# The second layer's conditioning map in a fused two-layer backbone kernel: products on ScalarE, sums of eight on GpSimd, the sum over partitions on TensorE

## The chip, the core and the metric

The kernel runs on one core of one Trainium2 chip. The metric is the device time of one execution in microseconds (us). The engines are named as the profile names them: PE is TensorE (PEld its weight loads), DVE is VectorE, ACT is ScalarE, POOL is GpSimd, SP is SyncE, which here only issues DMAs. "ACTq" is ACT's instruction queue: DMAs that ACT issues stand there, in order with its other work.

## The reference, cut to what matters

The program is one inference step of a two-layer backbone of width 1024, over 1024 latent and 128 context tokens. Each layer has a mixer (a convolution and Fourier mixer in layer 0, an S5 scan in layer 1) and a gated feed forward part; both are modulated by shift, scale and gate vectors, which come from the conditioning vector through one linear map per layer:

```
mod = jax.nn.silu(c_in) @ p['w_ada'][l] + p['b_ada'][l]      # (2 vectors, 1024) @ (1024, 6144)
sh1, sc1, g1, sh2, sc2, g2 = jnp.split(mod[:, None, :], N_MOD, axis=-1)
h = modulate(rmsnorm(x, p['norm1_g'][l]), sh1, sc1)           # h * (1 + scale) + shift
...                                                           # mixer, h -> m
x = x + g1 * m
h = modulate(rmsnorm(x, p['norm2_g'][l]), sh2, sc2)
x = x + g2 * swiglu(h, p['w_ffn_in'][l], p['w_ffn_out'][l])
```

There are two conditioning vectors: one for the latent tokens, one for the context tokens. The change concerns `mod` of the second layer (l = 1) and nothing else of the computation.

## The kernel before, in words

All products of activations and weights go through three fp32r matmuls of 384 columns on PE (`mm3`, lines 120 to 125): a weight tile is read by a DMA of SP's queue into `wraw`, ACT rounds it to `whi` (line 116), DVE takes the rest `wlo` (line 117), each with two buffers, and PE multiplies high by high, high by low and low by high. Results lie in six PSUM banks, which ACT or DVE empty.

Layer 0's feed forward is `ffn` (from line 603). `inner(j)` makes two weight tiles `wg` and `wu` and, for each of three chunks of 384 tokens, 24 matmuls with each; ACT takes silu of the first (line 619), DVE multiplies by the second (line 621), and the product is split in two (lines 153, 154). `outer(j0)`, after each second `inner`, multiplies back and DVE adds to the residual (line 599). The last pair, `last_outer`, goes a chunk at a time, so that the norm and then the modulated input of the S5 layer (`S5In.chunk`, lines 1020 to 1026, on ACT with shift and scale of layer 1) can start chunk by chunk.

Two other pieces of work ride along in `ffn`. They are a generator, `fill`: first the S5 tables' constants (`Tables.build`, 41 steps), then `table_steps` (from line 835), 8 tiles of 4 batches with 11 steps each and a step of `prepare` per tile, 360 steps. These are mostly short DVE operations with both inputs in SBUF (lines 831 to 833). `pump` (in `ffn`) advances the generator in proportion to the matmuls issued: 425 times the share of the work done. By the end of the loop over j that share is (4608 - 144) / 4752 = 0.94, so 400 steps have been taken; what is left is issued at once, ahead of `at_end()` and `last_outer`.

Inside the batches, layer 1's conditioning map is computed. Every seventh step `ada_rows` (lines 310 to 318) multiplies one block of 128 outputs: eight fp32 matmuls, 32 columns of `cond` (the two conditioning vectors, padded) stationary and 128 weight columns moving, four groups of products side by side. ACT copies the block's result to `arow`, issues its store to memory, and issues the load of the next block (`ada_load`, line 294, 512 KB in one buffer). After every six blocks `ada_sums` (lines 320 to 329) has ACT issue eight small DMAs, which bring the rows back as one output per partition, and POOL adds the four groups and the bias, giving `modt[1]`. There are 48 blocks and 8 sums. When the generator ends, POOL makes `scale_t[1]` (`ada_scale`, lines 332 and 334, called in lines 1726 and 1727).

Layer 0 has most of its own map computed the other way, in `ada_slice` (lines 265 to 284), before the feed forward: one product per slice and vector on ACT (line 274), the other seven accumulated on DVE (line 276), a matmul with `ones32` for the sum over partitions (line 280), rows through memory (line 284), `ada_columns` (lines 286 to 290) to bring them back.

What sets the order: within the program text, the order of the generators' steps. A planner then lays out every engine's instructions when the kernel is built, with program order as the priority; an instruction whose inputs or buffers are not ready in the plan lets later ones go ahead. On the chip each engine runs its list in order and waits where an input is late.

Of the kernel before, what the change touches and what calls it, by code (L numbers as in the profile page):

```python
# [38 lines left out]
SLOT = 8 * W  # L39


def segments(lo, hi):
    """the parts of a range of tokens by conditioning."""
    out = []
    if lo < LAT:
        out.append((lo, min(hi, LAT), 0))
    if hi > LAT:
        out.append((max(lo, LAT), hi, 1))
    return out
# [7 lines left out]
def kernel(  # L57
# [30 lines left out]
    # ---------------------------------------------------------------- constants  # L88
# [7 lines left out]
    ada1_d = dram.tile([128, 48 * 128], F32, name="ada1_d")  # L96
# [11 lines left out]
    # ---------------------------------------------------------------- helpers  # L108
# [24 lines left out]
    class Pools:  # L133
# [9 lines left out]
        def s(self, p, dt=F32):  # L143
            """short-lived tiles, apart from the long-lived ones where they have slots of their own."""
            return self.act.tile([128, CW], dt, tag="s", name=nm(p), bufs=self.ns) if self.ns else self.a(p, dt)
# [11 lines left out]
    # rsqrt(v) by Newton from an integer seed  # L157
# [17 lines left out]
    def unpermuted(fn, dst, src, ch):  # L175
        """context tokens back from (t, c) order."""
        if ch < NCH - 1:
            return fn(dst, src)
        n = LAT - ch * CW
        fn(dst[:, :n], src[:, :n])  # L180
        fn(dst[:, n:].rearrange("p (c t) -> p c t", t=T8), src[:, n:].rearrange("p (t c) -> p c t", t=T8))

    class Norm:
        """means of squares of a chunk's tokens, three blocks of tokens with one per partition."""
# [28 lines left out]
    def spread(r):  # L213
        """rstd of three blocks of tokens from a column per block to every partition."""
        rb, bw = aux("nrb"), r.shape[0]
        for j in range(3):
            PE.transpose(rb[:, j * bw:(j + 1) * bw], r[:, j:j + 1].to_broadcast([bw, 128]), ident[:bw, :bw])
        return rb

    def modulated_tile(P, x, rb, f, ch, l, which):  # L220
        """x * rstd * scale + shift of a tile, in its two parts; rb covers the chunk."""
        t, hi, lo = P.t("t"), P.h("hh", F32R), P.h("hl", F32R)
        c0 = ch * CW
        for a, b, s in segs(ch):
            cs = slice(a - c0, b - c0)
            sh = modt[l][:, 24 * which + f, s:s + 1]
            V.scalar_tensor_tensor(t[:, cs], x[:, a:b], scale_t[l][:, which, f, s:s + 1], rb[:, cs], op0=OP.mult, op1=OP.mult)
            S.activation(hi[:, cs], t[:, cs], AF.Identity, bias=sh)
            V.scalar_tensor_tensor(lo[:, cs], t[:, cs], sh, hi[:, cs].bitcast(F32), op0=OP.add, op1=OP.subtract)
        return hi, lo  # L230

    def modulated(P, norm, ch, xs, l, which, h):
        """in parts, a tile each."""
        rb = norm.scale(ch)
        for f in range(NF):
            h[f][ch] = modulated_tile(P, xs[f], rb, f, ch, l, which)
            yield
# [4 lines left out]
    # ---------------------------------------------------------------- conditioning  # L242
# [22 lines left out]
    def ada_slice(P, s):  # L265
        """a slice of layer 0's conditioning map, off the tensor engine but for the sum over partitions;
        in two parts, to be issued some time apart. The rows go through memory to one feature per partition."""
# [18 lines left out]
    def ada_columns(l, b0, nb, src, t):  # L286
        """blocks of 128 outputs, from memory to one per partition."""
        for i in range(2):
            nc.scalar.dma_start(t[:, i, :], src[i].rearrange("(b c) -> c b", c=128))
        V.tensor_add(modt[l][:, b0:b0 + nb, :], t.rearrange("p s b -> p b s"), vec_a[:, 48 * l + b0:48 * l + b0 + nb, None].to_broadcast([128, nb, 2]))  # L290
# [6 lines left out]
    def ada_block(pool, l, s, raw, nrow=2):  # L297
        """in two parts, to be issued some time apart."""
# [11 lines left out]
    def ada_rows(pool, s, raw):  # L310
        """a block of layer 1's conditioning map, the rows of the four groups of products to memory."""
        ps = aux("ada")
        for k in range(8):
            j = k % 4
            PE.matmul(ps[32 * j:32 * j + 32, :128], cond[:, k, :], raw[:, k, :], start=(k < 4), stop=(k >= 4))
        row = pool.tile([128, 128], F32, tag="arow", name=nm("arow"), bufs=2)
        S.activation(row, ps[:, :128], AF.Copy)
        nc.scalar.dma_start(ada1_d[:, s * 128:s * 128 + 128], row)

    def ada_sums(pool, b0, nb):  # L320
        """sums of the four groups, one output per partition."""
        t = pool.tile([128, 4, 2, nb], F32, tag="acol", name=nm("acol"), bufs=2)
        for j in range(4):
            for i in range(2):
                nc.scalar.dma_start(t[:, j, i, :], ada1_d[32 * j + i, b0 * 128:(b0 + nb) * 128].rearrange("(b c) -> c b", c=128))
        G.tensor_add(t[:, 0:2], t[:, 0:2], t[:, 2:4])
        G.tensor_add(t[:, 0], t[:, 0], t[:, 1])
        G.tensor_add(modt[1][:, b0:b0 + nb], t[:, 0].rearrange("p s b -> p b s"),
                     vec_a[:, 48 + b0:48 + b0 + nb, None].to_broadcast([128, nb, 2]))
# [13 lines left out]
    # ---------------------------------------------------------------- entry  # L343
    def start(P, st, x, h):
        """x to one feature per partition, its norm, modulation and the first two tiles of the
        input projection, a feature tile at a time as the conditioning arrives."""
# [96 lines left out]
    # ---------------------------------------------------------------- layer 0 mixer  # L443
    def mixer(P, big, x, h, norm2, hn, first):
# [10 lines left out]
        def four_in(i):  # L455
# [5 lines left out]
            # folded about 512 and 256: sums of even and odd outputs for cosine, then sine, and the middle  # L461
# [140 lines left out]
    # ---------------------------------------------------------------- feed forward  # L602
    def ffn(P, l, x, h, norm_next, steps=None, nsteps=0, at_end=None, per_chunk=None):
# [32 lines left out]
        def last_outer(j0):  # L636
            """the last two, a chunk of tokens at a time."""
# [25 lines left out]
    # ---------------------------------------------------------------- S5 tables  # L663
# [10 lines left out]
    def exp_poly(pool, x, n):  # L674
        """exp of an fp32 array by range reduction and a polynomial."""
# [21 lines left out]
    def sincos(pool, a, n):  # L697
        """sine and cosine of an fp32 array, reduced by parts of 2 pi that multiply exactly."""
# [36 lines left out]
    def state_layout(dst0, dst1, dup):  # L735
        """[(d, p), g] from dup[(d, g), p twice]."""
# [98 lines left out]
    def table_steps(P, pool, tb):  # L835
# [149 lines left out]
        raw, ns, summed, turn = ada_load(pool, 1, 0), 0, 0, 0  # L985
        for f in range(8):
            ct = prepare(f, *nxt)
            yield
            for q in range(4):
# [4 lines left out]
                for i, _ in enumerate(batch(f, q, ct, both)):  # L994
                    if ns % 6 == 0 and turn % 7 == 5 and summed < ns:
                        ada_sums(pool, summed, 6)
                        summed = ns
                    if turn % 7 == 0 and ns < 48:
                        ada_rows(pool, ns, raw)
                        ns += 1  # L1000
                        if ns < 48:
                            raw = ada_load(pool, 1, ns)
                    turn += 1
                    yield

    # ---------------------------------------------------------------- S5 layer
    class S5In:
        """modulated input of the S5 layer, a chunk of tokens at a time."""
# [24 lines left out]
    class S5:  # L1033
# [40 lines left out]
        def parts(f):  # L1074
            """the first and the last tile go through in halves."""
# [52 lines left out]
        def front(self, f):  # L1128
            """input products, chunk sums."""
# [43 lines left out]
        def back(self, f):  # L1173
            """outputs of the states, back to one feature per partition."""
# [73 lines left out]
    # ---------------------------------------------------------------- layer 1 after the scan  # L1248
# [6 lines left out]
    class Glu:  # L1255
        """gated output projection of the scan's outputs, half of the tokens at a time, in quarters."""
# [23 lines left out]
        def late(self, ws, cc):  # L1280
            """products of the first output, those with the last of the scan's outputs at the end."""
# [43 lines left out]
        def modulate(self, c):  # L1325
            """in place and in parts, a tile each."""
# [55 lines left out]
    class Fast:  # L1382
        """feed forward input product by seven products of half the features, tokens and outputs of a pair;
        for the first pair of outputs by eight."""
# [22 lines left out]
        def forms(self, s, h1, h2, tmp, eng):  # L1407
            """what the products take of two quarters of the tokens; in parts."""
# [40 lines left out]
        def weights(self, r):  # L1449
            """the seven weights in the order of the products."""  # L1450
# [43 lines left out]
        def plain(self, s, work):  # L1494
            """the first two outputs of half of the tokens."""
# [61 lines left out]
        def steps(self, j, up, tiles):  # L1557
            """a step per product of the outputs j and j + 1."""
# [8 lines left out]
            def done(n, s, src):  # L1567
                """an output to the hidden features."""
# [43 lines left out]
    class FfnOut:  # L1612
        """feed forward output product, a chunk of tokens at a time."""
# [85 lines left out]
    # ---------------------------------------------------------------- program  # L1699
# [138 lines left out]
```

## Time and profile before

| what | value |
|---|---|
| median of 3 runs (lowest to highest) | 2558.5 us (2555.06 to 2559.73) |
| profiled execution: its span, first to last instruction | 2550.3 us |
| what lies between that span and the median | 8.2 us |
| stage of the change (from the first load of layer 1's map to the end of the loop over j) | 480 to 1262 us of the span |
| handover to the S5 layer | 1262 to about 1320 us |

The profile gives, for one execution, when each engine was busy and what it waited for. Two things matter in reading it. The duration of a matmul is a modelled one and successive matmuls overlap, so that PE's pace is read from the distance between starts. And DVE and POOL instructions show longer durations when they were held up after they started, so a duration that is far above its usual value is a wait as well.

### The profile page before, as it was taken

The numbers are of one execution on the slowest core, as the hardware profiler recorded it, in microseconds if no ns is written. First come the engines' busy times: TensorE is split into PE (matmuls) and PEld (weight loads), VectorE is DVE, ScalarE is ACT, GpSimd is POOL, SyncE is SP. The second block draws the span as 40 slices with busy tenths as digits, with TensorE's granted clock in tenths as the row PEclk, the third lists the DMA queues.
The fourth block names the chain that finished last, engine by engine and source line by source line (L and its number), as shares of the span: only waits on it lengthen the run. The fifth ranks groups of instructions, "written<-read, shape, count | busy, mean of one in ns | idle before, by whom it ended". The sixth has DMA issues, their size and how long they took to land. (4 is left out here: it accounts for less than half of the span.)

```text
span 2550.3 us, 44262 instructions
## 1 busy us (share of the span) xinstructions
PE 2426.1 (95%) x16815; PEld 2360.4 (93%) x16815; DVE 1789.7 (70%) x4641; ACT 906.2 (36%) x1915; POOL 252.0 (10%) x256
## 2 busy tenths in 40 slices
PE   7999999999999999999956789999999999989998
PEld 6999999999999999999946679998999999989998
DVE  7765678787787778887869984558766666644444
ACT  5322443233222322223364443435232232434333
POOL 0000120000000000000124421112000000122110
PEclk9999999999999999999978889999999999999999
DMA  9443342244444444443457954433222222466543
GB/s 258 127 137 96 92 116 61 68 122 122 123 115 123 122 114 130 115 131 115 116 195 221 261 177 147 120 103 103 74 77 69 88 62 86 147 204 189 162 132 124
DMA packets 503093, 327.96 MB, mean 129 GB/s; under 512 B 99144, under 2 KB 472448, under 8 KB 502880
## 3 DMA queue, kind: packets, MB, share of 16 engines
q1 hardware_dynamic: 330208, 233.10, 30.8%
q10 hardware_dynamic: 163680, 58.96, 9.6%
q0 software_dynamic: 8992, 33.07, 3.9%
q8 instruction: 133, 2.18, 0.4%
q14 instruction: 80, 0.66, 0.1%
HBM read 254.04 MB, written 71.01 MB: 127 GB/s over the span
## 5 line engine op out<-in xcount | busy, mean ns | idle before, releaser
L123 PE MATMUL mm<-hh,whi 128*128 128x384 f32 x1392 | 472.6, 339 | 1.1 <-ACT f L459 1.1
L125 PE MATMUL mm<-hh,wlo 128*128 128x384 f32 x1392 | 466.4, 335 | 0.0
L124 PE MATMUL mm<-hl,whi 128*128 128x384 f32 x1392 | 465.3, 334 | 0.0
L117 DVE TENSOR_TENSOR wlo<-wraw,whi 128x1024 fp32r<-128x1024 f32 (+1 forms) x216 | 259.8, 1203 | 243.5 <-ACT whi L116 240.2
L116 ACT ACTIVATE whi<-wraw 128x1024 fp32r<-128x1024 f32 (+1 forms) x218 | 226.0, 1037 | 506.3 <-PE mm L124 383.5
L123 PEld LDWEIGHTS mm<-hh,whi 128*128 128x128 f32 x1392 | 261.3, 188 | 11.2 <-issue 9.2
L125 PEld LDWEIGHTS mm<-hh,wlo 128*128 128x128 f32 x1392 | 261.3, 188 | 2.9 <-issue 2.5
L124 PEld LDWEIGHTS mm<-hl,whi 128*128 128x128 f32 x1392 | 261.5, 188 | 0.0
L599 DVE SCALAR_TENSOR_TENSOR xall<-mm,modt,xall 128x384 f32<-128x384 f32 (+2 forms) x416 | 203.6, 510 | 60.3 <-PE mm L125 59.4
L123 PE MATMUL mm<-hb,whi 128*128 128x384 f32 x528 | 179.9, 341 | 11.3 <-ACT whi L116 11.2
L1534 PE MATMUL mm<-T,wf 128*128 128x288 f32 x640 | 189.4, 296 | 0.0
L1535 PE MATMUL mm<-T,wf 128*128 128x288 f32 x640 | 188.8, 295 | 0.0
L1536 PE MATMUL mm<-T,wf 128*128 128x288 f32 x640 | 188.2, 294 | 0.0
L125 PE MATMUL mm<-hb,wlo 128*128 128x384 f32 x528 | 179.4, 340 | 2.0 <-DVE wlo L117 1.9
L123 PE MATMUL mm<-hidh,whi 128*128 128x384 f32 x528 | 180.0, 341 | 0.0
L124 PE MATMUL mm<-hb,whi 128*128 128x384 f32 x528 | 178.6, 338 | 0.0
L125 PE MATMUL mm<-hidh,wlo 128*128 128x384 f32 x528 | 176.6, 334 | 0.0
L124 PE MATMUL mm<-hidl,whi 128*128 128x384 f32 x528 | 176.5, 334 | 0.0
L196 POOL TENSOR_TENSOR ssq<-ssq,sq 128x384 f32<-128x384 f32 (+1 forms) x78 | 100.1, 1284 | 686.9 <-ACT sq L192 683.7
L123 PE MATMUL mm<-zz,whi 128*128 128x288 f32 x512 | 151.5, 296 | 2.4 <-ACT zz L1267 2.4
L124 PE MATMUL mm<-zz,whi 128*128 128x288 f32 x512 | 150.8, 295 | 0.3
L125 PE MATMUL mm<-zz,wlo 128*128 128x288 f32 x512 | 150.4, 294 | 0.3 <-DVE wlo L117 0.3
(391 smaller groups left out, 5710.5 us busy)
## 6 DMA issues: line engine op xcount, KB each, us to landing
wraw<-in_w_ffn_out_dram SPq DMA_DIRECT2D x70, 512.0 KB
wraw<-in_w_ffn_in_dram SPq DMA_DIRECT2D x52, 512.0 KB
araw<-in_w_ada_dram ACTq DMA_DIRECT2D x48, 512.0 KB
wraw<-in_w_glu_dram SPq DMA_DIRECT2D x32, 512.0 KB
araw<-in_w_ada_dram ACTq DMA_DIRECT2D x80, 192.0 KB
wraw<-in_w_out_mix_dram SPq DMA_DIRECT2D x24, 512.0 KB
xall<-in_w_ffn_in_dram SPq DMA_DIRECT2D x20, 512.0 KB
wr<-in_w_ffn_in_dram SPq DMA_DIRECT2D x20, 512.0 KB
```

The source lines that it names most:

```text
L116: S.activation(hi[:, :n], raw[:, :n], AF.Copy)
L117: eng.tensor_sub(lo[:, :n], raw[:, :n], hi[:, :n].bitcast(F32))
L123: PE.matmul(ps, wh, xs[0], start=start, stop=False)
L124: PE.matmul(ps, wh, xs[1], start=False, stop=False)
L125: PE.matmul(ps, wl, xs[0], start=False, stop=stop)
L196: self.last = G.tensor_add(self.ssq[ch], self.ssq[ch], sq)
L599: V.scalar_tensor_tensor(x[o][:, a:b], ps[:, a - ch * CW:b - ch * CW], gate(l, which, o, s), x[o][:, a:b], op0=OP.mult, op1=OP.add)
L1534: PE.matmul(ps, wh, xh[:, cs], start=kt == 0, stop=False)
L1535: PE.matmul(ps, wh, xl[:, cs], start=False, stop=False)
L1536: PE.matmul(ps, wl, xh[:, cs], start=False, stop=kt == NFK - 1)
```

## The change

A generator `ada_pool` takes the place of `ada_load`, `ada_rows` and `ada_sums` for layer 1. It goes over 32 slices of 192 outputs. Each slice has eight steps: a load of 128 by 192 weights (96 KB, two buffers), two products on ACT (one per conditioning vector; `Copy` with a scale per partition), and, from the second step on, two additions on POOL into the accumulators. Then four empty steps, two matmuls with `ones32` for the sum over partitions, a copy on ACT and two row stores. One step of it is taken at each step of a batch. What is left of it is drained when the batches are through, one yield each; then one `ada_columns` brings back all 48 blocks, with the addition of the bias on DVE. `pump` and its count of 425 stay as they are.

```diff
+AW = 192
...
-    ada1_d = dram.tile([128, 48 * 128], F32, name="ada1_d")
+    ada1_d = dram.tile([2, 48 * 128], F32, name="ada1_d")
...
-    def ada_rows(pool, s, raw):
...
-    def ada_sums(pool, b0, nb):
...
+    def ada_pool(pool):
+        for c0 in range(0, 48 * 128, AW):
+            acc = [pool.tile([128, AW], F32, tag="acc", name=nm("acc"), bufs=2) for _ in range(2)]
+            for k in range(8):
+                raw = pool.tile([128, AW], F32, tag="araw", name=nm("araw"), bufs=2)
+                nc.scalar.dma_start(raw, w_ada[1, k * 128:(k + 1) * 128, c0:c0 + AW])
+                for i in range(2):
+                    if k == 0:
+                        S.activation(acc[i], raw, AF.Copy, scale=cond[:, 0, i:i + 1])
+                    else:
+                        t = pool.tile([128, AW], F32, tag="aprod", name=nm("aprod"), bufs=2)
+                        S.activation(t, raw, AF.Copy, scale=cond[:, k, i:i + 1])
+                        G.tensor_add(acc[i], acc[i], t)
+                yield
+            for _ in range(4):
+                yield
+            ps = aux("ada")
+            for i in range(2):
+                PE.matmul(ps[32 * i:32 * i + 32, :AW], ones32, acc[i], start=True, stop=True)
+            row = pool.tile([128, AW], F32, tag="aprod", name=nm("arow"), bufs=2)
+            S.activation(row[0:64], ps[0:64, :AW], AF.Copy)
+            for i in range(2):
+                nc.scalar.dma_start(ada1_d[i:i + 1, c0:c0 + AW], row[32 * i:32 * i + 1])
...
-        raw, ns, summed, turn = ada_load(pool, 1, 0), 0, 0, 0
+        ada = ada_pool(pool)
...
                 for i, _ in enumerate(batch(f, q, ct, both)):
-                    if ns % 6 == 0 and turn % 7 == 5 and summed < ns:
-                        ada_sums(pool, summed, 6)
-                        summed = ns
-                    if turn % 7 == 0 and ns < 48:
-                        ada_rows(pool, ns, raw)
-                        ns += 1
-                        if ns < 48:
-                            raw = ada_load(pool, 1, ns)
-                    turn += 1
+                    next(ada, None)
                     yield
+        for _ in ada:
+            yield
+        ada_columns(1, 0, 48, ada1_d, pool.tile([128, 2, 48], F32, tag="acol", name="acol1", bufs=1))
```

## Rows read from the trace of the kernel before

**Rows 1.** The page: the span, and busy time of each engine.

```profile
span 2550.3 us, 44262 instructions
PE 2426.1 (95%) x16815; PEld 2360.4 (93%) x16815; DVE 1789.7 (70%) x4641; ACT 906.2 (36%) x1915; POOL 252.0 (10%) x256
```

**Rows 2.** Busy time by stretch: PE, PEld, DVE, ACT, POOL; granted clock, DMA.

```profile
480.00:1262.00 782.00, 781.34 (x5543) 751.33 (x5542) 623.89 (x2414) 232.29 (x522) 7.83 (x28) 1.00 0.44 117
1262.00:1320.00 58.00, 34.72 (x210) 32.92 (x210) 39.56 (x97) 45.73 (x91) 26.10 (x39) 0.77 0.54 179
```

**Rows 3.** PE's waits, 300 to 1240 us: total, times, longest.

```profile
PE pk L953 <- ACT arow L317: 0.7, 1, 0.7
```

**Rows 4.** PE in order of time about one narrow block: start, us.

```profile
514.12 0.33 PE L124 MATMUL mm<-hl,whi 128*128 128x384 f32 x1
514.30 0.34 PE L125 MATMUL mm<-hh,wlo 128*128 128x384 f32 x1
514.57 0.65 PE L315 MATMUL ada<-araw,cond 128*32 128x128 f32 x16
515.14 0.44 PE L123 MATMUL mm<-hh,whi 128*128 128x384 f32 x1
```

**Rows 5.** PE in order of time about one sum of layer 0's map.

```profile
130.05 0.34 PE L125 MATMUL mm<-hh,wlo 128*128 128x384 f32 x1
130.32 0.84 PE L280 MATMUL ada<-acc,ones 128*32 128x384 f32 x4
131.09 0.45 PE L123 MATMUL mm<-hh,whi 128*128 128x384 f32 x1
```

**Rows 6.** Instructions on `ada` and `arow`: count, ns min/median/max, first and last start.

```profile
L315 PE MATMUL ada<-araw,cond x768: 272/273/298, 500.9 to 1216.9; 128*32 128x128 f32 x192
L317 ACT ACTIVATE arow<-ada x48: 256/278/324, 502.0 to 1217.2; 128x128 f32<-128x128 f32 x48
```

**Rows 7.** DVE by line, 480 to 1262 us: busy, mean ns, idle before.

```profile
L599 DVE SCALAR_TENSOR_TENSOR xall<-mm,modt,xall 128x384 f32<-128x384 f32 (+2 forms) x308 | 151.1, 510 | 4.2 <-PE mm L125 3.3
L621 DVE TENSOR_TENSOR sg<-sg,mm 128x384 f32<-128x384 f32 x57 | 31.4, 550 | 77.0 <-PE mm L125 66.5 <-PE ct L876 10.5
```

**Rows 8.** POOL in order of time: additions of 288 and of 384 columns.

```profile
1736.24 0.80 POOL L1421 TENSOR_TENSOR xall<-xall 128x288 f32<-128x288 f32 x1
...
1754.45 1.02 POOL L1421 TENSOR_TENSOR xall<-xall 128x288 f32<-128x288 f32 x1
...
1290.30 6.37 POOL L196 TENSOR_TENSOR ssq<-ssq,sq 128x384 f32<-128x384 f32 x6 [11.23 <-ACT sq L192]
```

**Rows 9.** DVE in order of time, 1752 to 1757 us.

```profile
1752.77 3.01 DVE L1405 TENSOR_TENSOR B<-xall,B 128x288 fp32r<-128x288 f32 x3
1755.71 1.55 DVE L1405 TENSOR_TENSOR T<-xall,T 128x288 fp32r<-128x288 f32 x4
```

**Rows 10.** ACT in order of time: layer 0's loads and the products behind them.

```profile
75.81 0.35 ACTq L271 DMA_DIRECT2D araw<-in_w_ada_dram  x1
...
78.92 0.62 ACT L274 ACTIVATE acc<-araw,cond 128x384 f32<-128x384 f32 x1 [2.67 <-DMA araw<-in_w_ada_dram]
```

**Rows 11.** A weight tile's two parts, on ACT and on DVE.

```profile
1205.37 1.06 ACT L116 ACTIVATE whi<-wraw 128x1024 fp32r<-128x1024 f32 x1 [3.34 <-PE mm L124]
...
1206.85 1.21 DVE L117 TENSOR_TENSOR wlo<-wraw,whi 128x1024 fp32r<-128x1024 f32 x1
```

**Rows 12.** The end of layer 1's map and S5's first inputs, on POOL and ACT.

```profile
1228.76 0.21 POOL L328 TENSOR_TENSOR modt<-acol,vec_a 128x12 f32<-128x12 f32 x1
...
1281.63 8.19 ACT L1025 ACTIVATE u<-t,modt,scalet 128x384 f32<-128x384 f32 x8
...
1307.67 10.08 ACT L1025 ACTIVATE u<-t,modt,scalet 128x256 f32<-128x256 f32 x16 [2.31 <-DVE t L1022]
```

**Rows 13.** Layer 0's columns brought back: their issue on ACT, the addition on DVE.

```profile
273.85 2.73 ACTq L289 DMA_DIRECT2D acol<-ada_d  x2
...
280.40 0.22 DVE L290 TENSOR_TENSOR modt<-acol,vec_a 128x60 f32<-128x60 f32 x1 [1.62 <-DMA acol<-ada_d]
```

More of the change, by code (lines that the diff above doesn't have):

```diff
@@ L308, in ada_block @@
         V.tensor_scalar(modt[l][:, s, :], po[:, 0:2], vec_a[:, 48 * l + s:48 * l + s + 1], None, op0=OP.add)
-    def ada_rows(pool, s, raw):
[L312 to L318, printed above, removed]
@@ L320, in ada_sums @@
-    def ada_sums(pool, b0, nb):
-        t = pool.tile([128, 4, 2, nb], F32, tag="acol", name=nm("acol"), bufs=2)
-        for j in range(4):
-            for i in range(2):
[L325 to L329, printed above, removed]
+    def ada_pool(pool):
[15 more added lines that the diff above has]
+            ps = aux("ada")
+            for i in range(2):
+                PE.matmul(ps[32 * i:32 * i + 32, :AW], ones32, acc[i], start=True, stop=True)
[3 more added lines that the diff above has]
+                nc.scalar.dma_start(ada1_d[i:i + 1, c0:c0 + AW], row[32 * i:32 * i + 1])
```

## The prediction

> **What bounds the kernel now.** I read the page of the profile first: PE is busy for 95% of the span, DVE for 70%, ACT for 36%, POOL for 10% [rows 1]. That invites moving work from PE to POOL. But an average over stages does not price this change, so the second view is the busy time of the stretch in which layer 1's map is made, 480 to 1262 us [rows 2]. There PE is busy for 781 of 782 us, ACT for 232, POOL for 8, and DVE for 624, which is 80%. Third, PE's waits in that stretch come to 0.7 us in all [rows 3]. So PE's own list of matmuls sets the time of the stage: what is taken from it is gained, and any lateness that outlasts the buffers is paid in full. Fourth, the end of the stage: `modt[1]` is complete at 1229 us, and the first instruction that needs it, the S5 input on ACT, starts at 1282 us [rows 12]. Before, the map was done 53 us early.
>
> **PE: what goes and what comes.** Around a narrow block the starts of the neighbours are 0.84 us apart (514.30 to 515.14), where neighbours are usually 0.18 apart [rows 4]: 0.66 us per block. There are 768 / 16 = 48 blocks [rows 6]: 31.7 us are removed. A sum over partitions of 384 columns took 130.05 to 131.09, less 0.18: 0.86 us [rows 5]. The new sums have 192 columns, so one costs between half of that, 0.43, and all of it; I take 0.48, near the half, as the passes are the same four. 29 of the 32 fall into the stage (below): 14 us, at most 25. Net: -17.7 us.
>
> A sum stands in PE's queue with all matmuls behind it, and it waits for POOL's last addition. Blocks stood seven steps apart, 502.0 to 1217.2 in 47 intervals [rows 6], so a step is 2.17 us. A slice has 12 steps, 26 us; its work (below) takes some 14 us and can begin once the previous sum has freed the accumulators. I put this wait at nothing; POOL's or ACT's slowing to half would uncover it.
>
> **POOL against DVE.** The 29 slices bring 406 additions of 192 columns to POOL. One of 288 columns took 0.80 us with nothing against it, six of 384 took 6.37, or 1.06 each with their gaps [rows 8]; on that line 192 columns take about 0.6. POOL has room for 244 us. The issue is what DVE does meanwhile. Three DVE operations with both inputs in SBUF took from 1752.77 to 1755.71 beside such additions, 0.98 each; the next four, with POOL idle, took 1.55, 0.39 each [rows 9]. POOL's additions show 1.02 instead of 0.80 there [rows 8]. So each addition of 0.80 took 0.59 from DVE, 74%; for 0.6 us that is 0.44.
>
> How often does DVE want its second input then? In the stage 151 us of line 599 and 31 of line 621 read one input from PSUM [rows 7]; the rest, 441 us, mostly has both inputs in SBUF, 56% of the time. If only this share of the additions hits, DVE loses 406 x 0.44 x 0.56 = 100 us; if every one does, 179. I take 0.7, 125 us, since the table operations follow each other closely and delayed ones bunch. DVE then needs 624 + 125 = 749 us of the 764 that PE would leave it: 98%. At the upper end it needs 803, and PE waits 39.
>
> The trace's pairs lose three quarters of the other's duration. The Trainium skill, SBUF — State Buffer, section "SBUF: two separate sides", states it more harshly: the pair of ports that VectorE and GpSimd share is held for a whole instruction and the other "fully blocks". By that, 0.6 in place of 0.44, DVE would lose 171 us, and the sum would end some 30 us higher; the rows decide.
>
> At 98%, in-order lists with few buffers do not run without waits. The tightest place is the weights: the tile that takes the freed buffer is needed after 24 matmuls, 24 x 0.174 = 4.2 us, and ACT's `whi` and DVE's `wlo` took 2.7 us from 1205.37 to 1208.06 [rows 11], so 1.5 us are left. `whi` now queues on ACT behind products, and `wlo` on DVE behind held-up table operations. Nothing in the trace prices that: nothing at the low end (a gain is excluded, PE waits for nothing now), 1 us for each of about 58 tiles at the high end. I take a third, 20 us, and half of DVE's 39: together **+40 us** in the stage, between 0 and 100.
>
> **ACT.** It loses 48 copies of 0.28 [rows 6] and gets 464 products. Of 384 columns one took 0.62 [rows 10]; 192 columns lie between 0.28 and that, say 0.4: 186 us. The loads, 8 a slice, cost 0.35 each to issue [rows 10]: 81 us. That makes 232 + 186 - 13 + 81 = 486 of 764 us, and the issues of the removed loads, stores and column loads (160 in all) roughly pay for what else it issues. 278 us are left, 1.2 us for each of 232 steps. A product can wait for its load (issued at 75.81, used at 78.92, 3.1 us for twice the bytes, two in flight [rows 10]) or for the addition that frees its buffer, and behind it in the queue wait silu, `whi` and the copies of the tables. I take this as covered by the 278 us, beyond the 20 us above. SP's and POOL's DMA queues get nothing new.
>
> **The handover.** After the change the generator has 41 + 360 + 32 = 433 steps: 352 batch steps carry 352 of the map's 384 steps, and the remaining 32 follow. The loop takes 400 steps, as before. Before, that left one; now it leaves all 32, issued at once before `last_outer`. Slices 29 to 31 therefore lie between the sum of slice 28, some three steps (6.5 us) before the end of the loop, and the first S5 input. A slice goes in four pairs of loads at about 3.1 us [rows 10] (POOL's four additions per pair, 2.4 to 2.8 us, fit), plus about 1.5 us for the sum: 14 us. Three are 42, less 6.5: 35. Then a row store and the columns: layer 0's 30 blocks took 6.6 us from issue to addition, 2.7 of it on ACT's queue [rows 13]; 48 take 6.6 to 10.5. With the copy, the store and the scales I put 12 us, so that `modt[1]` is ready at 1262 + 47 = 1309. ACT's three chunks then run without gaps, 8.2 + 8.2 + 10.1 = 26.5 us [rows 12], to 1335, where they ended at 1317.75: **+18 us**. It can be nothing, if the pieces overlap better and S5's own loads are what S5 waits for, and 35, if slices take 18 us and the 0.77 of granted clock there (a mean of the levels 1.2 and 2.4 GHz) [rows 2] lasts longer. DVE's addition of the columns may also hold the residual updates queued behind it; that is in the upper end. A gain is excluded, as nothing waited for `modt[1]`.
>
> **The sum.** The profiled execution spans 2550.3 us; 8.2 more make the median, and I carry these along. 2558.5 - 17.7 + 40 + 18 = 2599 us.
>
> **The rivals.** *PE is freed and DVE's idle time takes the rest.* For it: DVE idles 158 us in the stage, 77 of them ahead of line 621 waiting for PE [rows 7], and six banks of results let DVE lag. Then -17.7 and a handover of 3: 2544 us. Against it: 624 + 125 leaves 15 us. This is the case on the other side; it decides if additions hit DVE half as often as I take. The Trainium skill, Perfetto Trace Analysis, section "Identifying the Most-Contended Engine", says to relieve the engine with the highest occupancy first; here that is PE, and by that rule the time falls to this value.
>
> *The gain is given back at the handover.* Stage as in that rival, handover as in mine: 2558.5 - 17.7 + 18 = 2559 us. For it: the step count, which is arithmetic.
>
> *ACT becomes the bound.* It decides where a step makes ACT wait over 1.2 us. For it: two load buffers, two product buffers, and POOL's additions held by DVE. Against it: the planner moves products to where their inputs are there. At 1.6 us per step: 232 x 0.4 = 93 us in place of the 40: 2652 us.
>
> **How the numbers follow.** Chances: my forecast 0.48, freed PE 0.20, handover alone 0.13, ACT 0.19. About 0.2% (5 us) is what can be told from no change: 2553 to 2564. The first rival lies below it, the second within, the others above; with a little of each spilling over, 0.21, 0.14 and 0.65. The range of eight in ten takes in the first rival's value and ends short of its best case, and above it reaches past the ACT case: 2543 to 2665. My forecast alone runs from 2570 to 2640.
>
> **What would show it.** Right: narrow blocks gone and 64 sum matmuls in 32 pairs; PE's waits in the stage at tens of us, ended by `wlo`, `whi` or ACT; DVE above 90% busy there, with table operations of 256 and 128 columns longer than before; the first S5 input later than the end of the loop by some 45 us, ended by POOL's scales. Wrong: PE's waits still near zero and the stage some 18 us shorter (then the contention is overstated); the S5 input starting 20 us after the loop as now (then the map ran ahead of its place); or sums waiting for POOL's additions, which I took as covered.

## The result and the profile after

The changed kernel takes 2668.8 us (median of 4 runs, 2660.3 to 2671.9) against 2559.0 for the kernel before beside it: a ratio of 1.044, interval 1.0423 to 1.0461. That is slower, as forecast, but by 110 us instead of 40, and just above the range. Three marks cut a profiled execution into parts that add up to its span: the last silu of the loop over `j`, the first S5 input (`u` on ACT), the end. The table has the runs described below too.

| kernel | last silu at | silu to first `u` | first `u` to end | span | measured |
|---|---|---|---|---|---|
| before | 1255.5 | 26.1 | 1268.7 | 2550.3 | 2555 to 2559 |
| after | 1300.9 | 88.0 | 1279.9 | 2668.8 | 2668.8 |
| e1 map early | 1313.5 | 27.5 | 1276.0 | 2617.0 | 2619.9 |
| e2 faster steps | 1304.6 | 41.4 | 1276.8 | 2622.8 | 2626.8 |
| e3 no additions | 1237.5 | 83.8 | 1273.4 | 2594.7 | 2598.4 |
| e4 no products | 1295.4 | 87.3 | 1275.5 | 2658.2 | 2665.7 |
| e5 early, no additions | 1249.6 | 27.7 | 1278.5 | 2555.8 | 2555.1 |
| e9 early, half of the additions | 1290.6 | 27.6 | 1275.6 | 2593.8 | 2593.5 |
| e7 early, on DVE | 1312.6 | 27.9 | 1267.8 | 2608.2 | 2609.6 |
| e6 other queues | 1300.5 | 79.3 | 1274.7 | 2654.6 | 2653.5 |
| e8 wider blocks | 1258.6 | 26.1 | 1269.0 | 2553.8 | 2556.9 |
| e11 24 blocks later | 1236.8 | 27.4 | 1357.0 | 2621.2 | 2623.1 |
| e12 the same, loads earlier | 1239.1 | 27.0 | 1312.8 | 2578.9 | 2582.0 |
| e13 12 blocks later | 1250.5 | 26.0 | 1293.7 | 2570.2 | 2576.0 |

Of the 118.5 us between the two spans, 45.4 arise in the loop, 61.9 behind it, and 11.2 after the first S5 input.

**The loop.** Busy time by stretch of the kernel after, as in [rows 2]:

```profile
480.00:1262.00 782.00, 744.93 (x4631) 713.29 (x4630) 669.17 (x2264) 379.98 (x921) 263.17 (x388) 0.98 0.37 104
480.00:1300.00 820.00, 780.48 (x4825) 747.17 (x4823) 705.92 (x2390) 395.82 (x955) 276.50 (x406) 0.98 0.36 104
1300.00:1420.00 120.00, 45.61 (x264) 40.37 (x263) 45.60 (x121) 62.10 (x128) 51.65 (x85) 0.66 0.36 91
```

TensorE is no longer busy throughout. DVE is busy for 706 of 820 us: more than before, but 86%, not the forecast 98%. The granted clock is 0.98 where it was 1.00; 2% of 820 is some 16 us, an estimate of what the clock costs. The third line is the way to the S5 layer: TensorE is busy for 46 of 120 us there. PE's waits, 480 to 1310 us (total, times, longest), in place of the 0.7 us of [rows 3]:

```profile
PE mm L126 <- DVE wlo L118: 26.6, 16, 3.3
PE mm L124 <- ACT whi L117: 6.7, 5, 3.2
PE et L921 <- DVE e L839: 2.9, 3, 1.8
```

So the weights are late, `wlo` above all. Groups of POOL and DVE in the same stretch (busy, mean ns):

```profile
L325 POOL TENSOR_TENSOR acc<-acc,aprod 128x192 f32<-128x192 f32 x406 | 276.5, 699 | 628.5 <-ACT aprod L324 620.5 <-PE pk L959 6.3
L118 DVE TENSOR_TENSOR wlo<-wraw,whi 128x1024 fp32r<-128x1024 f32 x56 | 68.6, 1225 | 17.6 <-ACT whi L117 17.5
L839 DVE TENSOR_TENSOR e<-e,tm 128x256 f32<-128x256 f32 x64 | 32.0, 500 | 0.1
L605 DVE SCALAR_TENSOR_TENSOR xall<-mm,modt,xall 128x384 f32<-128x384 f32 x154 | 92.9, 607 | 4.1 <-PE mm L126 4.0
```

and two of them in the kernel before, 480 to 1262 us:

```profile
L833 DVE TENSOR_TENSOR e<-e,tm 128x256 f32<-128x256 f32 x64 | 26.8, 418 | 0.2
L599 DVE SCALAR_TENSOR_TENSOR xall<-mm,modt,xall 128x384 f32<-128x384 f32 x154 | 93.2, 610 | 2.3 <-PE mm L125 1.7
```

The table operations, with both inputs in SBUF, have grown (this group from 418 to 500 ns); the residual updates, which read one input from PSUM, have not (610 and 607). `wlo` itself takes no longer than in [rows 11] (1.21 us), though both its inputs lie in SBUF. What makes it late stands ahead of it on DVE. One case in order of time, all engines, with the lines that matter:

```profile
951.42 1.10 ACT L117 ACTIVATE whi<-wraw 128x1024 fp32r<-128x1024 f32 x1
...
951.78 0.48 DVE L837 TENSOR_TENSOR fx<-ct,pf 128x320 f32<-128x320 f32 x1
...
953.31 2.98 POOL L325 TENSOR_TENSOR acc<-acc,aprod 128x192 f32<-128x192 f32 x4 [2.15 <-ACT aprod L324]
...
953.46 0.88 DVE L837 TENSOR_TENSOR e<-pe,bb 128x256 f32<-128x256 f32 x1
...
954.26 0.83 DVE L839 TENSOR_TENSOR fx<-fx,tm 128x320 f32<-128x320 f32 x1
...
955.02 0.81 DVE L839 TENSOR_TENSOR e<-e,tm 128x256 f32<-128x256 f32 x1
...
955.75 0.88 DVE L914 TENSOR_TENSOR tm<-ct,pf 128x320 f32<-128x320 f32 x1
...
956.55 1.21 DVE L118 TENSOR_TENSOR wlo<-wraw,whi 128x1024 fp32r<-128x1024 f32 x1
...
957.82 0.69 PE L126 MATMUL mm<-hh,wlo 128*128 128x384 f32 x1 [3.11 <-DVE wlo L118]
...
958.31 0.52 PE L124 MATMUL mm<-hh,whi 128*128 128x384 f32 x1
...
958.63 0.52 PE L125 MATMUL mm<-hl,whi 128*128 128x384 f32 x1
```

Without an addition beside it an operation on 320 columns takes 0.48, and the two kinds on 256 columns 0.61 and 0.42; the four between 953.46 and 956.6, beside four additions, take 0.8 to 0.9 each. `wlo`, whose `whi` began at 951.42, starts 5.1 us later, where the pair of [rows 11] stands 1.5 us apart. PE waits 3.11 us, and then its matmuls start 0.32 us apart instead of the 0.18 of [rows 4]: that is the lower clock level, 1.2 GHz, with a granted clock of 0.50 from 957.8 to 960.0 us.

**Behind the loop.** ACT, POOL and DVE in order of time, in place of [rows 12]:

```profile
1302.59 0.31 ACT L333 ACTIVATE arow<-ada 64x192 f32<-64x192 f32 x1
...
1321.54 0.33 ACT L333 ACTIVATE arow<-ada 64x192 f32<-64x192 f32 x1 [1.38 <-PE ada L331]
...
1336.62 0.32 ACT L333 ACTIVATE arow<-ada 64x192 f32<-64x192 f32 x1 [1.47 <-PE ada L331]
...
1355.44 0.32 ACT L333 ACTIVATE arow<-ada 64x192 f32<-64x192 f32 x1 [1.81 <-PE ada L331]
...
1356.91 7.48 ACTq L290 DMA_DIRECT2D acol<-ada_d  x2
...
1368.20 0.52 ACT L193 ACTIVATE ssq<-xall 128x384 f32<-128x384 f32 x1 [12.44 <-issue]
...
1370.03 0.26 DVE L291 TENSOR_TENSOR modt<-acol,vec_a 128x96 f32<-128x96 f32 x1 [34.71 <-DMA acol<-ada_d]
...
1370.38 0.37 POOL L338 TENSOR_SCALAR scalet<-modt 128x16 f32<-128x16 f32 x2 [15.88 <-DVE modt L291]
...
1372.22 8.38 POOL L197 TENSOR_TENSOR ssq<-ssq,sq 128x384 f32<-128x384 f32 x8
...
1388.93 4.02 ACT L1026 ACTIVATE u<-t,modt,scalet 128x384 f32<-128x384 f32 x4 [3.14 <-DVE t L1023]
```

The three slices left over end 19, 15 and 19 us apart. Then come the columns, until 1370. Only then does the norm of the S5 input begin: its squares stand on ACT behind the columns' loads and a load of the S5 state (3.7 us), its sums on POOL behind the scales, though the residual updates were finished by 1335. The norm takes another 18.9 us.

### The profile page after: what moved, and what is told of

It reads as the page before. It is cut to its first block, busy times and chain, and to the rows that moved or that the text cites. A ratio compares the mean times of both kernels' runs of the same rounds, so it can differ in the third digit from the quotient of the medians.

```text
span 2668.8 us, 44316 instructions
## 1 busy us (share of the span) xinstructions
PE 2443.3 (92%) x16175; PEld 2371.4 (89%) x16175; DVE 1879.2 (70%) x4642; ACT 1095.3 (41%) x2411; POOL 537.0 (20%) x680
## 5 line engine op out<-in xcount | busy, mean ns | idle before, releaser
L126 PE MATMUL mm<-hh,wlo 128*128 128x384 f32 x1392 | 472.4, 339 | 23.0 <-DVE wlo L118 23.0
L325 POOL TENSOR_TENSOR acc<-acc,aprod 128x192 f32<-128x192 f32 x448 | 301.7, 691 | 661.6 <-ACT aprod L324 653.2
L126 PEld LDWEIGHTS mm<-hh,wlo 128*128 128x128 f32 x1392 | 264.6, 190 | 30.1 <-DVE wlo L118 27.4
L324 ACT ACTIVATE aprod<-araw,cond 128x192 f32<-128x192 f32 x448 | 189.6, 449 | 150.4 <-DMA araw<-in_w_ada_dram 76.0
L124 PE MATMUL mm<-zz,whi 128*128 128x288 f32 x512 | 152.7, 299 | 3.3 <-ACT zz L1268 3.3
```

The source lines that it names most:

```text
L124: PE.matmul(ps, wh, xs[0], start=start, stop=False)
L126: PE.matmul(ps, wl, xs[0], start=False, stop=stop)
L324: S.activation(t, raw, AF.Copy, scale=cond[:, k, i:i + 1])
L325: G.tensor_add(acc[i], acc[i], t)
```

## The experiments

**e1: the map early.** Two empty steps a slice instead of four, and the columns read back by the map itself, so that no slice is left over.

```diff
-            for _ in range(4):
+            for _ in range(2):
                 yield
...
+        ada_columns(1, 0, 48, ada1_d, pool.tile([128, 2, 48], F32, tag="acol", name="acol1", bufs=1))
...
-        ada_columns(1, 0, 48, ada1_d, pool.tile([128, 2, 48], F32, tag="acol", name="acol1", bufs=1))
```

> Edit: two empty steps per slice instead of four, and the columns are brought back at the end of the generator itself. 320 steps instead of 384, so the map is complete some 30 batch steps (60 us or more) before the loop over j ends, and nothing of it is left for the handover; the contention of POOL, ACT and DVE inside the loop stays. Theory A (the map's leftover of 32 steps and its column load stand in front of everything at the handover and cost some 62 of the 110 us): the last silu to the first S5 input falls from 88 us to about 26, the span from 2669 to about 2607. Rival B (the 62 us come from engines that lag at the loop's end through contention, whatever is left): handover stays above 60 us and the time above 2650.

2619.9 us, ratio 1.0254 [1.0236, 1.0273]. The way from the last silu to the first `u` is 27.5 us, as before. The leftover slices and the columns behind them are thus the whole loss behind the loop; 12.6 us of it return in the loop, which is denser.

**e2: the steps taken faster**, 461 counted instead of 425, with the slices as in the change.

```diff
-                ffn(P, 0, x, h, n3, fill(), 425, at_end, per_chunk)
+                ffn(P, 0, x, h, n3, fill(), 461, at_end, per_chunk)
```

> Edit: the count that paces the generator raised from 425 to 461, so that all 433 steps are taken inside the loop. The map then ends just at the loop's end instead of 32 steps after it, and only the last sum, the store and the column load remain. Theory A: the handover falls from 88 us to 40 to 50 (the column load still stands behind the last sum), the time to about 2630; the steps come 8% closer in time, so the stage itself may lose up to 10 us more. Rival B: 2660 or more.

2626.8 us, ratio 1.0279 [1.0254, 1.0304], and 41.4 us behind the loop: a second way to the same finding, with the columns alone still late, some 15 us.

**e3: no additions on POOL.**

```diff
-                        G.tensor_add(acc[i], acc[i], t)
```

> Leaves out the 448 additions on POOL, so the map is that of the first 128 of 1024 inputs; loads, products on ACT and sums on PE stay. Theory C (the stage's loss is POOL's additions holding DVE's two-input operations): PE's waits inside the loop fall from about 40 us to under 12 and the slower-clock stretches go with them; the loop ends 40 to 60 us earlier than in the changed kernel. Rival D (the stage's loss is ACT's added work and its waits for loads): PE's waits stay above 25 us. Both expect the handover somewhat shorter, since a slice's chain is shorter without additions: 60 to 80 us instead of 88.

2598.4 us, ratio 1.0168 [1.0143, 1.0192]. Its loop is 18.0 us *shorter* than before. Busy time, 480 to 1242 us:

```profile
480.00:1242.00 762.00, 760.94 (x4874) 735.71 (x4873) 621.47 (x2411) 393.22 (x969) 0.00 (x0) 1.00 0.39 112
```

and the longest of PE's waits in it:

```profile
PE mm L126 <- DVE wlo L118: 0.7, 1, 0.7
```

The loads, the products on ACT and the sums are all still there, and TensorE is busy throughout again. So the saving of 17.7 us is real, and POOL's additions are what eats it. Behind the loop the run takes 83.8 us, more than the 60 to 80 expected.

**e4: no products on ACT**; POOL adds the weights themselves.

```diff
-                        S.activation(t, raw, AF.Copy, scale=cond[:, k, i:i + 1])
-                        G.tensor_add(acc[i], acc[i], t)
+                        G.tensor_add(acc[i], acc[i], raw)
```

> Leaves out the 448 products on ACT: POOL adds the raw weights to the accumulators, so the map has wrong factors; loads, additions and sums stay. Theory C (POOL against DVE): DVE stays above 88% busy in the stage and PE's waits stay at 25 us or more; the loop's end moves by less than 15 us. Rival D (ACT): PE's waits fall under 12 us and the loop ends 40 to 60 us earlier.

2665.7 us, ratio 1.0431 [1.0396, 1.0466]: what the whole change costs, with ACT back at 245 of 820 us. The loop ends 5.5 us earlier than in the changed kernel. ACT's load is not the cause, and neither is that the additions keep ACT's products waiting for their buffers, as no such product is left.

**e5: e1 and e3 together.**

> Leaves out the 448 additions on GpSimd, so most of the map's products are lost; the two late slices are issued inside the loop as well. Theory: the whole loss is the sum of two parts, GpSimd's additions holding VectorE in the loop (run without additions: the loop's last product of the feed forward came 17.1 us earlier than in the kernel before) and the three slices behind the loop (run with the map early: the way from the last silu to the first S5 input was 27.5 us, as before). If nothing else is in it, both parts taken out leave TensorE's saving alone: 2556 - 17 = about 2539 to 2543 us. Rival, a third cost that neither run showed (ScalarE's products and loads, at some 400 us of its time, or the row stores): 2550 us or more.

2555.1 us, ratio 1.0003 [0.9992, 1.0015]: both losses gone, yet no gain. The loop ends 5.9 us earlier than before, not 18. So the denser order by itself costs 12.1 us in the loop (e5 against e3), as it does with the additions (12.6, e1 against the changed kernel). Three more sums in it are some 1.6 us of that, and ACT's copies of the tables come late at times (one wait of 2.8 us); the rest is not assigned. After the first `u` this execution is 9.8 us longer than the one of before. Some 8 of them lie before layer 1's feed forward, where TensorE waits for the S5 stage's own transfers (`U`: 30.5 us, 23.0 before). All that stretch lies between 1267.8 and 1279.9 in the table where the S5 stage has no blocks, and the runs of the kernel before spread over 13 us by themselves (2549 to 2562), so a single profile can't tell whether the change causes it. That part of the third cost stays open.

**e9: e1 with every second slice's additions left out.**

```diff
-                        G.tensor_add(acc[i], acc[i], t)
+                        if c0 // AW % 2:
+                            G.tensor_add(acc[i], acc[i], t)
```

> The map early in the loop, with the additions of every second slice left out: 224 of 448. All of them cost 65 us (2619.9 against 2555.1 without any). Theory that VectorE has idle time to give first and TensorE is held up only once that is used up: half of the additions cost far less than half, 2555 to 2570. Rival, that each addition does its harm where it lands, by making one weight tile or one table operation late: the cost goes by their number, 2582 to 2595.

2593.5 us, ratio 1.0145 [1.0117, 1.0172]. The first 224 additions cost 38.4 us, the next 224 another 26.4: no stock of idle time is used up first. The loop's busy time without additions, in e5:

```profile
480.00:1253.00 773.00, 767.17 (x4886) 737.83 (x4885) 622.52 (x2412) 409.57 (x1013) 1.59 (x9) 1.00 0.40 113
```

with half of them, in e9:

```profile
480.00:1294.00 814.00, 785.40 (x4892) 749.75 (x4891) 674.47 (x2412) 415.36 (x1014) 152.83 (x236) 0.98 0.38 108
```

and with all, in e1:

```profile
480.00:1317.00 837.00, 789.88 (x4889) 747.61 (x4888) 722.51 (x2412) 420.00 (x1014) 312.21 (x460) 0.98 0.37 105
```

DVE's instructions are the same 2412 and take 52 and 100 us longer: 0.23 and 0.22 us per addition. The last silu moves by 41 and 64 us. DVE is busy for 81, 83 and 86%; PE loses most of what DVE loses, although DVE idles 114 us even in e1. Not all of PE's loss comes through DVE: in this denser order a sum also waits for POOL's last addition, 6.0 us in e9 and, in e1,

```profile
PE ada L331 <- POOL acc L325: 8.7, 11, 1.6
```

**e7: e1 with each product and addition as one operation on DVE.**

```diff
-                        S.activation(t, raw, AF.Copy, scale=cond[:, k, i:i + 1])
-                        G.tensor_add(acc[i], acc[i], t)
+                        V.scalar_tensor_tensor(acc[i], raw, cond[:, k, i:i + 1], acc[i], op0=OP.mult, op1=OP.add)
```

> The map early in the loop as in that run (2619.9), but each product and its addition are one operation on VectorE, with nothing on GpSimd and ScalarE. VectorE gets 448 operations of 192 columns, about 0.3 us each by the 0.39 of the 288-column operations of layer 1's norm: 134 us, on the 633 that it needs in the loop without additions. If GpSimd's additions cost just what they take from VectorE, and VectorE's own work would take no less: 2615 to 2650. If an addition on GpSimd costs more than the same arithmetic done on VectorE (because it holds up the in-order list at bad moments): below 2612.

2609.6 us, ratio 1.0209 [1.0187, 1.0231], 10 us less than e1. Its operations by line (min/median/max):

```profile
L323 DVE SCALAR_TENSOR_TENSOR acc<-araw,cond,acc x448: 401/414/432, 491.7 to 1244.2; 128x192 f32<-128x192 f32 x150
```

and the loop's busy time:

```profile
480.00:1316.00 836.00, 798.87 (x4892) 750.57 (x4891) 755.45 (x2860) 251.64 (x566) 1.60 (x9) 0.98 0.37 105
```

An operation shows 0.41 us, but they overlap, and against e5 DVE's busy time rises by 133 us, 0.30 for each, as expected. The time falls into the second of the two ranges, but not through the loop, which is as long as e1's (last silu at 1312.6 and 1313.5); the gap between the two lies after the first `u`, which the profiles can't assign. In the loop an addition on POOL and the whole operation on DVE do equal harm.

**e6: the order behind the loop**, in the changed kernel.

```diff
-            nc.scalar.dma_start(t[:, i, :], src[i].rearrange("(b c) -> c b", c=128))
+            (nc.sync if l else nc.scalar).dma_start(t[:, i, :], src[i].rearrange("(b c) -> c b", c=128))
...
-                    ada_scale(1, 0, G)
-                    ada_scale(1, 1, G)
+                    ada_scale(1, 0)
+                    ada_scale(1, 1)
```

> The changed kernel with two things moved behind the loop: the two column loads go out from SyncE's queue instead of ScalarE's, and the four scale operations run on VectorE instead of GpSimd. Theory that the order in the lists of ScalarE and GpSimd is part of the handover: the norm's squares on ScalarE and their sums on GpSimd no longer stand behind the map's columns and scales, and run beside the last products; of the 88 us from the last silu to the first S5 input some 18 go (the way from the scales at 1370 to the first input at 1389), to about 70, and the time falls to about 2650. Rival, that the three slices of 15 to 19 us alone set it and the norm would be late anyway, or that the squares wait for residual updates held behind the columns' addition on VectorE: 85 to 90 us and 2663 to 2670.

2653.5 us, ratio 1.0383 [1.0354, 1.0412]; the time fell as expected, the way to `u` only to 79.3, not 70. ACT, POOL and DVE in order of time:

```profile
1352.48 0.52 ACT L193 ACTIVATE ssq<-xall 128x384 f32<-128x384 f32 x1 [1.02 <-DMA ada_d<-arow]
...
1361.65 0.26 DVE L291 TENSOR_TENSOR modt<-acol,vec_a 128x96 f32<-128x96 f32 x1 [25.23 <-DMA acol<-ada_d]
...
1361.97 0.22 POOL L1039 MEMSET smask<- 128x146 f32 x1 [11.78 <-DVE modt L291]
...
1363.15 8.39 POOL L197 TENSOR_TENSOR ssq<-ssq,sq 128x384 f32<-128x384 f32 x8
```

The squares start 16 us earlier. Their sums start only 9 us earlier: with the scales gone, a memset of the S5 stage stands next on POOL and still waits for `modt`. That comes 8 us earlier, as the last slice ends 4 us sooner and the columns' issues take 3.9 us on SyncE's queue instead of 7.5. This gave nearly all of the 8.7 us, and the norm still takes 18 us behind `modt`. That it would go if POOL's list were free as well is argued from these rows, not shown.

**e8: wider narrow blocks**, from the kernel before: half of the inputs and 256 outputs per step, four products of 256 columns instead of eight of 128.

```diff
-        for k in range(8):
-            j = k % 4
-            PE.matmul(ps[32 * j:32 * j + 32, :128], cond[:, k, :], raw[:, k, :], start=(k < 4), stop=(k >= 4))
+        for j in range(4):
+            PE.matmul(ps[32 * j:32 * j + 32, :256], cond[:, n % 2 * 4 + j, :], raw[:, j, :], start=True, stop=True)
```

> The kernel before, with its narrow products on TensorE in another shape: 256 outputs and half of the inputs at a time instead of 128 outputs and all inputs, so four products of 256 columns in four column groups per step instead of eight of 128 in two rounds; the halves are added on GpSimd with the columns. Same bytes per load. Theory that a block's 0.66 us on TensorE hold a part that goes by the number of products (eight issues): 48 steps of 0.45 to 0.55 us, 5 to 10 us less, 2546 to 2551. Rival, that only columns count (512 columns in four groups either way): 2556, no difference. Against both, ScalarE's copies are of 256 instead of 128 columns (about 0.1 us more each).

2556.9 us, ratio 1.0009 [0.9998, 1.002]: no difference that can be told. PE about one of its blocks:

```profile
513.77 0.34 PE L125 MATMUL mm<-hh,wlo 128*128 128x384 f32 x1
514.03 0.64 PE L321 MATMUL ada<-araw,cond 128*32 128x256 f32 x8
514.60 0.45 PE L123 MATMUL mm<-hh,whi 128*128 128x384 f32 x1
```

The neighbours start 0.83 us apart, as in [rows 4] (0.84). The blocks' price does not go by the number of products.

**e11 to e13: half of the blocks elsewhere.** Only 24 of the 48 narrow blocks are read by the S5 layer's input and gate. From the kernel before, e11 makes the others among the S5 products, called between its steps:

```diff
-                    if turn % 7 == 0 and ns < 48:
+                    if turn % 14 == 0 and ns < 24:
...
+        def more(self):
+            if self.ns < 48:
+                ada_rows(self.ada, self.ns, self.raw)
+                self.ns += 1
+                if self.ns < 48:
+                    self.raw = ada_load(self.ada, 1, self.ns)
```

> The kernel before, with all products of the map on TensorE as there, but only the first 24 blocks (the norm and gate of the S5 layer) in the loop; the other 24, which are first read after the scan, are made among the S5 products. If a block costs its 0.66 us where TensorE is busy without a break and nearly nothing where it waits for DMAs (between 1300 and 1400 us it is busy for 59 of 100): 24 x 0.66 = 16 us less, and up to 6 us of that given back where a block delays an S5 product or its load delays a table: 2539 to 2546. Rival, that the S5 stage is bound by its transfers, and 24 loads of 512 KB there delay it by 2 us or more each: 2556 or more.

> The map split between the loop (24 blocks) and the S5 stage (24 blocks) as before, but in the S5 stage the weights are loaded two blocks ahead into two buffers, and the columns are read back later. In the split run the loop came out 18.7 us shorter, and TensorE then waited 80.9 us in the S5 stage for the blocks' loads. Theory that only the lateness of a load started one block ahead was paid there: those waits go to under 20 us and the time to 2540 to 2560. Rival, that the stage's transfers themselves are the bound and 12.6 MB more take their time whenever they start: 2590 or more.

> The same with 36 blocks in the loop and 12 in the S5 stage, one in some 16 us. The loop gives 12 x 0.66 = 8 us. Lateness theory: no wait for loads is left, 2545 to 2552. Rival (transfers are the bound): half of the loss of the 24-block form, 2565 to 2590.

e11 takes 2623.1 us (1.027 [1.0246, 1.0295]), e12 2582.0 (1.0102 [1.0085, 1.0119]), e13 2576.0 (1.0089 [1.006, 1.0117]). In e11 the last silu is 18.7 us earlier (16 were expected): what a block costs in the loop is gained. More than that is lost in the S5 stage. PE's waits of e11, 1235 to 1620 us:

```profile
PE ada L315 <- DMA araw<-in_w_ada_dram: 80.9, 15, 11.4
```

and those of e12, with loads two ahead:

```profile
PE ada L316 <- DMA araw<-in_w_ada_dram: 56.0, 10, 15.0
```

Loads two ahead save 41 us against e11, so lateness was part of the loss; but e12 lies in neither of its ranges, below the rival's 2590 and above 2560. Busy time of the end of e12's S5 stage and of the same stretch in the kernel before, the DMA share in the last column but one:

```profile
1400.00:1520.00 120.00, 79.12 (x729) 73.40 (x728) 100.33 (x76) 40.74 (x147) 39.66 (x23) 0.80 0.98 243
1400.00:1520.00 120.00, 92.89 (x699) 88.70 (x698) 113.15 (x96) 46.56 (x158) 45.33 (x24) 0.87 0.78 224
```

The DMA engines are busy for 98% of that stretch in e12, 78% before: there the 12.6 MB more fill them. In e11 and e13 the share is 83% and 82%, though TensorE waits 80.9 and 24.6 us for the blocks' loads; how much of their loss is lateness and how much the transfers, these runs do not separate. No version here beats the kernel before.

## Why the prediction was right in sign and wrong in size

**PE's saving, -17.7 us:** right. e3's loop is 18.0 us shorter. A sum cost 0.54 us (about the one at 971.91 us the neighbours start 0.72 apart, less 0.18) where I took 0.48. The sums did not wait for POOL in the changed kernel, as taken.

**ACT, covered:** right; e4 takes ACT's products away and the time stays. A product takes 0.45 us instead of the 0.4 that I took. The rival in which ACT becomes the bound (2652 us) was near the measured time for the wrong reason.

**POOL against DVE, 125 us taken from DVE, 98% busy:** the direction right, the size too high. An addition took 0.70 us; DVE's busy time in the loop rose from the 621 us of e3, without additions, to 711 (480 to 1305), 89 for some 406 additions, 0.22 each where I took 0.31. The Trainium skill (SBUF — State Buffer, section "SBUF: two separate sides") states that the engine that comes second "fully blocks" for the whole instruction. By that rule, and if every addition met such an operation, an estimate is that 406 x 0.70 = 284 us would be held; the trace shows a third of it, and no run here tells how many additions met one.

**The stage, +40 us:** mis-sized. It lost 45.4 + 17.7 = 63 us. The working split it into an overload of DVE (20, half of the 39 of its upper end) and late weights (20). There was no overload at 86%. PE's waits in the rows above come to 36 us, 33 of them for weight tiles; the clock after such waits costs some 16 more; the other 11 I have not assigned. The step that failed is the use of DVE's idle time as cover, by which 40 of the 125 us taken from DVE reached PE; measured, PE lost 63 where DVE lost 89. e9 shows that the cost goes by the number of additions from the first half on. DVE's idle time lies where DVE waits for PE or ACT, not where `wlo` needs it.

**The handover, +18 us:** this is the term that failed most; it measured 61.9. Right were the leftover of 32 steps and that the S5 input waits for the map (e1). Wrong were three sizes. Slices took 15 to 19 us instead of 14, and the columns' issues 7.5 us of ACT's queue instead of about 4 (2.7 for 30 blocks, scaled to 48), so `modt` was ready 65 us after the loop's last product (1305.7) instead of the 50 that 1309 means from 1259: 15 us. I let the S5 input start the moment `modt` was ready; the norm, which I didn't follow in the lists of ACT and POOL, came behind it: 19 us. And I let its three chunks run without gaps, 26.5 us; they took 36.8, since the norm of each was just as late: 10 us. 18 + 15 + 19 + 10 = 62. Of the signs named ahead, the waits ended by `wlo` came; DVE above 90% did not, and the S5 input was later than named and was ended by the norm, not by POOL's scales.

**After the first S5 input, nothing:** 11.2 us in these two profiles, not settled (e5).

**The rivals.** The freed PE (2544 us) fell: the loop lost 63 us with the additions in it, and even without one addition and without a leftover slice e5 is at 2555. By the Trainium skill's rule (Perfetto Trace Analysis, section "Identifying the Most-Contended Engine") PE was the engine to relieve first. The trace agrees that PE bounds the loop (781 of 782 us busy), but the work then lay on GpSimd, whose additions hold up VectorE, and VectorE makes PE's weights. The handover alone (2559) fell as well, since e1, which has none of it, is still 64 us above the kernel before.

## What to carry to other kernels

Work moved to GpSimd can be paid by VectorE (here 0.22 us for each addition of 0.70), and where VectorE splits the weights for a TensorE without waits, each of its delays can reach TensorE, however much idle time the average shows. Before a generator is given more steps, count what is left over at its end, and follow in every engine's list what then stands behind the leftover, not only who reads its result. Before using an engine's idle time, ask what it idles for: TensorE idled in the S5 stage for transfers, and blocks moved there brought more of them, up to a DMA share of 98% in e12.

## What the runs showed of the hardware that was not expected

A wait of 3 us is not only 3 us: after the one at 957.82 TensorE's matmuls started 0.32 us apart instead of 0.18, at a granted clock of 0.50, and the granted clock of the loop fell to 0.98. Beside GpSimd's additions VectorE's operations with both inputs in SBUF grew (418 to 500 ns), those with one input in PSUM did not (610 and 607), and `wlo`, with both in SBUF, did not either. Four products of 256 columns cost TensorE as much as eight of 128 with the same bytes (e8). And 448 operations of 0.41 us on VectorE itself lengthened the loop no more than 448 additions of 0.70 us on GpSimd beside it (e7), though they raised VectorE's busy time by 133 instead of 100 us.
